# A convolution's last tap applied to the block and to the running sum, and an evacuation and weight casts issued behind the last square

## The chip, the cores and the metric

One core of one Trainium2 chip runs the whole kernel; no other core takes part. The metric is the device time of one execution in microseconds (us). Each time shown is the median of several runs. One further execution was recorded by the hardware profiler; its page and its trace are what the text quotes. In them PE is TensorE's matrix unit, PEld its loading of weights, DVE is VectorE, ACT is ScalarE, POOL is GpSimd and SP is SyncE, which issues the DMAs. "L1501" is line 1501 of the kernel.

## The reference

The input is one sequence of 1024 tokens with 1024 channels. Layer 0 (a state space model beside retention) is not touched. Layer 1 is a gated Conformer convolution, with the norms around it:

```
def mixer_conv(h, w_in, conv_w, conv_b, ln_g, ln_b, w_out):
    proj = h @ w_in
    a, b, g = jnp.split(proj, 3, axis=-1)
    u = a * jax.nn.sigmoid(b)
    u = lax.conv_general_dilated(u, conv_w[:, None, :], ...)     # causal, depthwise, width CONV_K = 31
    u = u + conv_b
    mu = jnp.mean(u, axis=-1, keepdims=True)
    var = jnp.mean(jnp.square(u - mu), axis=-1, keepdims=True)
    u = (u - mu) * lax.rsqrt(var + EPS) * ln_g + ln_b
    u = jax.nn.silu(u) * jax.nn.silu(g)
    return u @ w_out

x = x + mixer_conv(rmsnorm(x, norm_g[1]), ...)
out = rmsnorm(x, final_g)
```

Everything is float32. The mean and the variance are taken over all 1024 channels of a token, so the last of the channels must be through the convolution before any of them can be normalised.

## The kernel before

**Layout.** Channels lie on the 128 partitions and time on the free axis. The 1024 channels make 8 blocks (KB), and the 1024 tokens are worked on as two halves of 512 (HALF), so that a tile is 128 x 512. A product in float32 is done as three products of a reduced type: each operand is split into a high and a low part, and `mm3` multiplies high weights by high data (L181), high weights by low data (L182) and low weights by high data (L183). One output block of 128 x 512 takes 8 steps of three matmuls, 24 in all, into one PSUM bank. There are three such banks ("mm"). The high part of a block of weights is cast on ScalarE (L171, or L148 where a block is loaded a second time) and the low part is a subtraction on GpSimd (L172), or for the second half a load of what the first half stored. Weights are fetched two blocks ahead (`wnext`), three buffers for each part.

**What runs around the change.** The end of the kernel has these pieces, for the first half (h = 0) and the second (h = 1):

- `conv(h, n2)`: the taps of two blocks. A few go to ScalarE and GpSimd (L1477, L1478); the others are instructions of VectorE (L1501), each of which multiplies a shifted slice of `u` by a weight per channel and adds it to an accumulator in a bank. For blocks 4 to 7 an estimate of the mean, `pilot`, is subtracted ahead of the last tap (L1494). The last tap writes its result to a tile `co` in SBUF.
- `conv_sums`: GpSimd adds the blocks up, one sum over the values (`cs`, L1542) and one over their squares (`cq`, L1544), each a 128 x 512 tile. ScalarE makes the squares (`csquare`).
- `conv_norm`: for the second half VectorE adds block 7 to the sum (L1551) and block 7's square, which ScalarE leaves in a bank `cvq_bank`, to the sum of squares (L1552). `conv_norm_wide` then sums each over the partitions with one product with a matrix of ones (`wide_sums`, L487), which leaves the two statistics `cst0` and `cst1` in two banks, spread over all partitions. The variance (L1584, L1588), the mean (L1587) and the reciprocal root (`wide_rsqrt`: a table load L495, Ln L497, Exp L498 and Square L499 on ScalarE, L500 and L501 on VectorE) follow.
- `conv_scale`: per block the value is scaled, the mean's part subtracted, Silu applied (L1605 on ScalarE), the gate multiplied in (L1611), and the result split into `zh` (a cast on ScalarE, L1232) and `zl` (a subtraction, L1234). The eight pairs are the operands of the second half's output products.
- `w_out_c(h, nb)`: one output block: 24 matmuls into a bank `mm_oc`, the evacuation on VectorE that adds the residual (L1635), its square on ScalarE (L1636), the sum of squares on GpSimd (L1640) and a scaling on ScalarE (L1641).

**What sets the order.** A scheduler places each engine's instructions by priorities (`self.at(n)`, the lower number first) and by when their inputs are there; `self.tc.issue_after(ins)` adds an edge, so that what is inside is issued behind `ins`. Each engine then works through its own queue in order. The output blocks of the first half fill TensorE while the second half's norm is on the other engines: blocks 0 to N0 - 1 are emitted ahead of it. Blocks N0 to 7 are emitted behind it, with `hold`: a dictionary that says from which of the 8 steps on a block's matmuls are issued behind a given instruction. Here `norm_mm`, the second statistic, stands between steps 0 and 1 of block 5:

```
N0, HOLD = 5, 1
...
    def gemm_seq(self, ps, seq, hold=None):
        with ExitStack() as held:
            for i, (w, xs, kb) in enumerate(seq):
                if hold and i in hold:
                    held.enter_context(self.tc.issue_after(hold[i].ins))
                self.mm3(ps, w, kb, (xs[kb][0][:], xs[kb][1][:]), i == 0, i == len(seq) - 1)
```

The functions that the diff touches, and what calls them:

Of the kernel before, what the change touches and what calls it, by code (L numbers as in the profile page):

```python
# [11 lines left out]
F32 = mybir.dt.float32  # L12
F32R = mybir.dt.float32r
I32 = mybir.dt.int32
AF = mybir.ActivationFunctionType
ALU = mybir.AluOpType
# [3 lines left out]
P = 128  # L20
D = 1024
T = 1024
KB = 8
HALF = 512
NH = 8
EPS = 1e-6
CONV_K = 31
MAGIC = 12582912.0
N0, HOLD = 5, 1
WARM = 14  # L30
RMM = 5
IDLE = 4
# [20 lines left out]
class Trunk:  # L53
# [1182 lines left out]
    def layer0_back_and_layer1(self, st):  # L1236
        nc, A = self.nc, self.A
        v, gp = nc.vector, nc.gpsimd
# [3 lines left out]
        ps_cv = self.pool("ps_cv", 2, PSUM, stack=st)  # L1242
# [96 lines left out]
        for i, x in ((6, t2), (7, t3), (4, t4)):  # L1339
            for m in range(2):  # L1340
                w = wn()
# [122 lines left out]
        def conv(h, n2):  # L1464


            accs_, outs, us, s0s = [], [], [], []
            late = h == 0 and n2 == 0
            for nb in (n2, n2 + 1):
                u = ub[h][nb]  # L1470
                with self.at(105000 + 100000 * h + 100 * nb):
                    s0 = lp.tile([P, HALF], F32, name=f"tp{nb}_{h}_0", tag="tp", bufs=3)
                    nc.scalar.activation(s0[:], u[:, 0:HALF], AF.Identity, scale=cw[:, nb, 0:1],
                                         bias=self.vec(V_CB, nb))
                    for k in range(1, NT[h]):
                        sk = lp.tile([P, HALF], F32, name=f"tp{nb}_{h}_{k}", tag="tp", bufs=3)
                        nc.scalar.mul(sk[:], u[:, k:k + HALF], cw[:, nb, k:k + 1])  # L1477
                        gp.tensor_tensor(s0[:], s0[:], sk[:], op=ALU.add)  # L1478
                us.append(u)
                s0s.append(s0)  # L1480
                acc = ps_cv.tile([P, HALF], F32, name=f"cv{nb}_{h}", tag="cv")
                if not late:
                    with self.at(105000 + 100000 * h + 100 * nb):
                        nc.scalar.copy(acc[:], s0[:])  # L1484
                accs_.append(acc)
                outs.append(opB.tile([P, HALF], F32, name=f"co{nb}_{h}", tag="B0"))
            for k in range(NT[h], CONV_K):
                for i, nb in enumerate((n2, n2 + 1)):
                    dst = outs[i] if k == CONV_K - 1 else accs_[i]
                    tap = us[i][:, k:k + HALF], cw[:, nb, k:k + 1]  # L1490
                    if k == CONV_K - 1 and late:
                        v.tensor_tensor(accs_[i][:], accs_[i][:], s0s[i][:], op=ALU.add)
                    if k == CONV_K - 1 and n2 >= 4:
                        v.tensor_tensor(accs_[i][:], accs_[i][:], pilot[h][:], op=ALU.subtract)  # L1494

                    ahead = (h, n2) == (0, 6) and k >= NORM_TAP[i]
                    if k == NT[h] and late:
                        v.tensor_scalar(dst[:], *tap, None, op0=ALU.mult)
                        continue
                    with self.tc.issue_after(self.norm_first.ins) if ahead else nullcontext():  # L1500
                        v.scalar_tensor_tensor(dst[:], *tap, accs_[i][:], op0=ALU.mult, op1=ALU.add)  # L1501
            cv[h][n2:n2 + 2] = outs
# [14 lines left out]
        def csquare(h, nb, bank=None):  # L1517
            sq = bank or (self.opA.tile([P, HALF], F32, name=f"cvq{nb}_{h}", tag="A1") if h else
                  lp.tile([P, HALF], F32, name=f"cvq{nb}_{h}", tag="sq", bufs=1))
            nc.scalar.activation(sq[:], cv[h][nb][:], AF.Square)  # L1520
            return sq

        def conv_center(h):
# [21 lines left out]

        def conv_norm(h):
            sm, acc = accs[("cv", h)]

            q7 = csquare(h, 7, h and ps_cv.tile([P, HALF], F32, name="cvq_bank", tag="cv"))
            e = v if h else gp  # L1550
            e.tensor_tensor(sm[:], sm[:], cv[h][7][:], op=ALU.add)  # L1551
            e.tensor_tensor(acc[:], acc[:], q7[:], op=ALU.add)  # L1552
            if h:
                return conv_norm_wide(sm, acc)
            st = ps_cv.tile([P, HALF], F32, name=f"cst_{h}", tag="cn")
            s1, s2 = st[:, 0:256], st[:, 256:512]
            self.token_sums([(s1, sm[:]), (s2, acc[:])])
            st4 = st[:].rearrange("p (k b x) -> p k b x", k=2, x=64)

            t4 = [lp.tile([P, 4], F32, name=f"cn4_{i}_{h}", tag=f"cn4_{i}", bufs=1) for i in range(4)]  # L1560
            d4, q4, v4, r4 = (t[:] for t in t4)
            nc.scalar.activation(q4, st4[:, 0, :, 0], AF.Square, scale=1.0 / D)
            nc.scalar.mul(d4, st4[:, 0, :, 0], 1.0 / D)
            v.scalar_tensor_tensor(v4, st4[:, 1, :, 0], 1.0 / D, q4, op0=ALU.mult, op1=ALU.subtract)
            self.rsqrt(r4, v4)
            v.tensor_tensor(d4, d4, r4, op=ALU.mult)
            Rp = ps_cv.tile([P, HALF], F32, name=f"cR_{h}", tag="cn")
            self.spread_split(Rp[:], r4, lp, f"cR_{h}")
            Dp = ps_cv.tile([P, HALF], F32, name=f"cD_{h}", tag="cn")
            with self.tc.issue_after(self.last_diag.ins):  # L1570
                self.spread_split(Dp[:], d4, lp, f"cD_{h}")
            dl = lp.tile([P, HALF], F32, name=f"dl_{h}", tag="cs", bufs=1)
            nc.scalar.copy(dl[:], Dp[:])
            conv_scale(h, Rp, dl)

        def conv_norm_wide(sm, acc):

            s1, s2 = (ps_cv.tile([P, HALF], F32, name=f"cst{i}_1", tag="cn") for i in range(2))
            self.wide_sums(s1[:], sm[:])
            self.wide_sums(s2[:], acc[:])  # L1580
            self.norm_mm = self.last_stat

            m2 = lp.tile([P, HALF], F32, name="cm2_1", tag="dg", bufs=1)
            self.squared = nc.scalar.activation(m2[:], s1[:], AF.Square, scale=1.0 / D)  # L1584
            dl = lp.tile([P, HALF], F32, name="dl_1", tag="cs", bufs=1)
            with self.tc.issue_after(self.squared.ins):
                nc.scalar.mul(dl[:], s1[:], 1.0 / D)  # L1587
            v.scalar_tensor_tensor(s2[:], s2[:], 1.0 / D, m2[:], op0=ALU.mult, op1=ALU.subtract)  # L1588
            self.wide_rsqrt(s2[:], lp, "cn_1")
            v.tensor_tensor(dl[:], dl[:], s2[:], op=ALU.mult)  # L1590
            conv_scale(1, s2, dl)
# [23 lines left out]
                zs[h][nb] = (a, b)  # L1615

        final = [[], []]

        def w_out_c(h, nb, cols, hold=None):

            w = self.wnext(f"woc{nb}_{h}")
            tag, bufs = ("tp", 3) if h and nb > 4 else ("ld", 2)
            xt = lp.tile([P, HALF], F32, name=f"x1l{nb}_{h}", tag=tag, bufs=bufs)
            with self.tc.issue_after(self.early_low.ins) if h and nb > 4 else nullcontext():
                nc.sync.dma_start(xt[:], self.x1_d[rows(nb), hs(h)])
            t = self.opA.tile([P, HALF], F32, name=f"x2_{nb}_{h}", tag=f"A{h}")
            sq = lp.tile([P, HALF], F32, name=f"s2q{nb}_{h}", tag="sacc" if nb == 0 else "ev",
                         bufs=1 if nb == 0 else 3)
            final[h].append((t, sq))

            def part(c):
                ps = self.bank(f"mm_oc{nb}_{h}_{c.start}", aux=False)
                n = c.stop - c.start
                self.gemm(ps[:, :n], w, [(a[:, c], b[:, c]) for a, b in zs[h]], hold)
                self.last_add = v.tensor_tensor(t[:, c], ps[:, :n], xt[:, c], op=ALU.add)  # L1635
                self.squared = nc.scalar.activation(sq[:, c], t[:, c], AF.Square)  # L1636

                if 0 < nb < KB - (h == 1 and c.start > 0):
                    a = final[h][0][1]
                    gp.tensor_tensor(a[:, c], a[:, c], sq[:, c], op=ALU.add)  # L1640
                nc.scalar.mul(t[:, c], t[:, c], self.vec(V_FG, nb))  # L1641
            for c in cols:
                yield part(c)
# [49 lines left out]
        for h in range(2):  # L1693
# [15 lines left out]
            def blocks(h, nbs, hold={}):  # L1709
                for nb in nbs:  # L1710
                    for _ in w_out_c(h, nb, full, hold.get(nb)):
                        pass

            with self.at(400000):
                if h == 0:
                    blocks(0, range(N0))
                    continue
                blocks(0, range(N0, 8), {N0: {HOLD: self.norm_mm}, N0 + 1: {0: self.norm_mm}})
            with self.at(410000):
                blocks(1, range(3))  # L1720
                with self.tc.issue_after(self.last_mm.ins):
# [123 lines left out]
```

## Time and profile before

| | before |
|---|---|
| median of three runs | 1184.66 us (1184.64 to 1185.43) |
| the profiled execution | 1186.61 us |
| its span | 1184.8 us |
| PE (TensorE) busy | 1171.0 us, 99% of the span |
| DVE (VectorE) busy | 847.0 us, 71% |
| POOL (GpSimd) busy | 655.4 us, 55% |
| ACT (ScalarE) busy | 490.0 us, 41% |
| mean granted clock of TensorE | 0.996 |

How to read the rows that follow. A row of single instructions gives start, duration, engine, line, operation, output<-inputs, the tile's shape and type, and in brackets how long the engine was idle ahead of it and what ended that wait; "x5" stands for five like instructions in a row. In the chain of waits each row is a start, a share of time and the engine, tile and line that the end of the program waited for then. In the view by stretches each engine has its busy time with the count of instructions; PEclk is the granted clock of TensorE, as a share of full speed. A busy PE is not PE at its peak: at a lower clock the same matmul is busy for longer.

### The profile page before, as it was taken

To read this page: it belongs to the slowest core of one execution; us is meant where nothing else is said; L and a number is where in the kernel's file an instruction comes from. 1 tells how busy PE (TensorE), PEld (TensorE's weight loads), DVE (VectorE), ACT (ScalarE), POOL (GpSimd) and SP (SyncE) were. 2 spreads that over 40 slices of the span, in tenths; PEclk is the share of its full clock that TensorE was granted. 3 is DMA by queue.
4 is the path that set the end of the run, shared out by engine and by line. 5 is a ranking of instruction groups with operands and counts; after the bars stand their busy time and mean duration, and the time that the engine had idled before them with its cause. 6 is when DMAs were issued, how large, how long until landed. Compare 5 with 4: busy or idle time off the path is not lost.

```text
span 1184.8 us, 17218 instructions
## 1 busy us (share of the span) xinstructions
PE 1171.0 (99%) x6286; PEld 979.9 (83%) x6286; DVE 847.0 (71%) x1463; ACT 490.0 (41%) x719; POOL 655.4 (55%) x448
## 2 busy tenths in 40 slices
PE   9999999999999999999999999999999999999897
PEld 7888888888888889999888888888888888888676
DVE  7975698777417359586679324599999799899643
ACT  6422232322223231333456325445536675344673
POOL 2059999888145354233572111687525577667643
PEclk9999999999999999999999999999999999999899
DMA  9344345555387667779998977656668554367664
GB/s 350 107 135 136 126 153 170 183 174 187 109 279 259 246 224 210 248 230 361 366 340 288 322 269 237 220 196 215 223 224 303 199 203 142 110 212 272 207 243 148
DMA packets 117637, 261.46 MB, mean 221 GB/s; under 512 B 10672, under 2 KB 42288, under 8 KB 116912
## 3 DMA queue, kind: packets, MB, share of 16 engines
q1 hardware_dynamic: 117552, 260.36, 65.0%
q8 instruction: 49, 0.80, 0.3%
q14 instruction: 36, 0.29, 0.1%
HBM read 181.48 MB, written 74.65 MB: 216 GB/s over the span
## 4 chain that ended last, share of the span: by engine, by line
PE 89%; DMA 3%; DVE 3%; ACT 1%; issue 1%; POOL 1%; SPq 1%; POOLq 0%; DVEq 0%; ACTq 0%
PE mm_g L181 8%; PE mm_g L182 7%; PE mm_g L183 7%; PE mm_wo L182 5%; PE mm_wo L183 5%; PE mm_wo L181 5%; PE mm_b L182 2%; PE mm_a L182 2%; PE mm_b L181 2%; PE mm_a L181 2%; PE mm_b L183 2%; PE mm_a L183 2%; PE mm_glu L181 2%; PE mm_glu L182 2%; PE mm_glu L183 2%; PE mm_oc L182 2%
## 5 line engine op out<-in xcount | busy, mean ns | idle before, releaser
L1501 DVE SCALAR_TENSOR_TENSOR cv<-u,convw,cv 128x512 f32<-128x512 f32 x398 | 273.1, 749 | 11.6 <-ACT cv L1484 9.7
L1478 POOL TENSOR_TENSOR tp<-tp,tp 128x512 f32<-128x512 f32 x64 | 83.8, 1309 | 36.5 <-ACT tp L1477 35.5
L181 PE MATMUL mm_g<-xh,wh_g 128*128 128x512 f32 x256 | 101.8, 398 | 0.0
L183 PE MATMUL mm_g<-xh,wl_g 128*128 128x512 f32 x256 | 100.1, 391 | 0.0
L182 PE MATMUL mm_g<-xl,wh_g 128*128 128x512 f32 x256 | 100.0, 391 | 0.0
L415 POOL TENSOR_TENSOR s1q<-s1q,s1q 128x512 f32<-128x512 f32 x12 | 17.7, 1477 | 86.1 <-ACT s1q L410 86.1
L1477 ACT ACTIVATE tp<-u,convw 128x512 f32<-128x512 f32 x64 | 45.3, 718 | 34.7 <-POOL tp L1478 34.6
L181 PEld LDWEIGHTS mm_g<-xh,wh_g 128*128 128x128 f32 x256 | 48.0, 188 | 11.7 <-issue 1.2
L183 PEld LDWEIGHTS mm_g<-xh,wl_g 128*128 128x128 f32 x256 | 48.1, 188 | 10.4
L182 PEld LDWEIGHTS mm_g<-xl,wh_g 128*128 128x128 f32 x256 | 48.1, 188 | 9.9 <-issue 0.4
L371 DVE TENSOR_TENSOR gt<-mm_g,R 128x512 f32<-128x512 f32 x32 | 21.8, 683 | 45.5 <-PE mm_g L183 45.5
L181 PE MATMUL mm_oc<-zh,wh_woc 128*128 128x512 f32 (+1 forms) x144 | 53.9, 379 | 0.0
L182 PE MATMUL mm_oc<-zl,wh_woc 128*128 128x512 f32 (+1 forms) x144 | 53.1, 370 | 0.2 <-POOL zl L1234 0.2
L183 PE MATMUL mm_oc<-zh,wl_woc 128*128 128x512 f32 (+1 forms) x144 | 52.8, 369 | 0.0
L172 POOL TENSOR_TENSOR wl_v<-wf_v,wh_v 128x1024 fp32r<-128x1024 f32 x12 | 31.2, 2611 | 38.5 <-ACT wh_v L171 38.5
L172 POOL TENSOR_TENSOR wl_glu<-wf_glu,wh_glu 128x1024 fp32r<-128x1024 f32 x14 | 34.0, 2428 | 33.0 <-ACT wh_glu L171 26.6
L181 PE MATMUL mm_wo<-ysh,wh_wos 128*128 128x512 f32 x128 | 50.2, 392 | 0.0
L181 PE MATMUL mm_g<-h1h,wh_cg 128*128 128x512 f32 x128 | 50.2, 392 | 0.0
L183 PE MATMUL mm_b<-h1h,wl_cb 128*128 128x512 f32 x128 | 49.9, 390 | 0.0
L182 PE MATMUL mm_b<-h1l,wh_cb 128*128 128x512 f32 x128 | 49.8, 389 | 0.0
L182 PE MATMUL mm_wo<-ysl,wh_wos 128*128 128x512 f32 x128 | 49.8, 389 | 0.0
L182 PE MATMUL mm_a<-h1l,wh_ca 128*128 128x512 f32 x128 | 49.8, 389 | 0.0
(523 smaller groups left out, 3652.5 us busy)
## 6 DMA issues: line engine op xcount, KB each, us to landing
wf_g<-w_ab SPq DMA_DIRECT2D x16, 512.0 KB
wf_wos<-w_out SPq DMA_DIRECT2D x16, 512.0 KB
wf_wor<-w_out SPq DMA_DIRECT2D x16, 512.0 KB
wf_cb<-w_c SPq DMA_DIRECT2D x16, 512.0 KB
wf_ca<-w_c SPq DMA_DIRECT2D x16, 512.0 KB
wf_woc<-w_out_c SPq DMA_DIRECT2D x16, 512.0 KB
wf_v<-w_v SPq DMA_DIRECT2D x12, 512.0 KB
wf_cg<-w_c SPq DMA_DIRECT2D x11, 512.0 KB
```

What stands on the lines that cost most here:

```text
L172: self.low_made = lo[i].tensor_tensor(wl[:].rearrange(fl)[:, c], wf[:, c], h.bitcast(F32), op=ALU.subtract)
L181: nc.tensor.matmul(ps, wh[:, kb, :], xh, start=start, stop=False, **more)
L182: nc.tensor.matmul(ps, wh[:, kb, :], xl, start=False, stop=False, **more)
L183: self.last_mm = nc.tensor.matmul(ps, wl[:, kb, :], xh, start=False, stop=stop, **more)
L371: nc.vector.tensor_tensor(gt[:, c], ps[:], self.R[:, c], op=ALU.mult)
L415: nc.gpsimd.tensor_tensor(a, a, sq[:], op=ALU.add)
L1477: nc.scalar.mul(sk[:], u[:, k:k + HALF], cw[:, nb, k:k + 1])
L1478: gp.tensor_tensor(s0[:], s0[:], sk[:], op=ALU.add)
L1501: v.scalar_tensor_tensor(dst[:], *tap, accs_[i][:], op0=ALU.mult, op1=ALU.add)
```

## The change

The change does four things, all of them near the second half's norm.

- The last tap of the second half's block 7 is no longer issued in `conv`. Its operands are kept in `self.last_tap`, and `conv_norm_wide` issues three instructions of VectorE: `total` = accumulator + old sum, into a bank (`cvs_bank`); `co` = tap + accumulator, as before; and the new sum = tap + `total`. The last tap is thus applied twice, to the block and to the sum. The sum's addition of `co` (L1551) goes. The square of block 7 and its addition follow, and that addition is remembered as `squares_added`.
- N0 goes from 5 to 4: block 4 of the first half is emitted behind the norm, without a hold. Its evacuation is issued behind `squares_added`.
- Blocks 5 to 7 of the first half (their loads and casts with them, as far as they are fetched there) are issued behind ScalarE's square of block 7, `last_square`.
- HOLD goes from 1 to 2: the second statistic stands between steps 1 and 2 of block 5, and ahead of block 6.

For the first half the statements are only moved within `conv_norm`.

```diff
-N0, HOLD = 5, 1
+N0, HOLD = 4, 2
...
+                    if (h, nb, k) == (1, KB - 1, CONV_K - 1):
+                        self.last_tap = *tap, accs_[i], dst
+                        continue
...
-            nc.scalar.activation(sq[:], cv[h][nb][:], AF.Square)
+            self.squared = nc.scalar.activation(sq[:], cv[h][nb][:], AF.Square)
...
-            q7 = csquare(h, 7, h and ps_cv.tile([P, HALF], F32, name="cvq_bank", tag="cv"))
-            e = v if h else gp
-            e.tensor_tensor(sm[:], sm[:], cv[h][7][:], op=ALU.add)
-            e.tensor_tensor(acc[:], acc[:], q7[:], op=ALU.add)
             if h:
                 return conv_norm_wide(sm, acc)
+            q7 = csquare(h, 7)
+            gp.tensor_tensor(sm[:], sm[:], cv[h][7][:], op=ALU.add)
+            gp.tensor_tensor(acc[:], acc[:], q7[:], op=ALU.add)
...
         def conv_norm_wide(sm, acc):
+            u, w, part, co = self.last_tap
+            total = ps_cv.tile([P, HALF], F32, name="cvs_bank", tag="cv")
+            v.tensor_tensor(total[:], part[:], sm[:], op=ALU.add)
+            v.scalar_tensor_tensor(co[:], u, w, part[:], op0=ALU.mult, op1=ALU.add)
+            v.scalar_tensor_tensor(sm[:], u, w, total[:], op0=ALU.mult, op1=ALU.add)
+            q7 = csquare(1, 7, ps_cv.tile([P, HALF], F32, name="cvq_bank", tag="cv"))
+            self.last_square = self.squared
+            self.squares_added = v.tensor_tensor(acc[:], acc[:], q7[:], op=ALU.add)
...
-                self.last_add = v.tensor_tensor(t[:, c], ps[:, :n], xt[:, c], op=ALU.add)
+                behind = self.behind.pop(nb, None)
+                with self.tc.issue_after(behind.ins) if behind else nullcontext():
+                    self.last_add = v.tensor_tensor(t[:, c], ps[:, :n], xt[:, c], op=ALU.add)
...
-                blocks(0, range(N0, 8), {N0: {HOLD: self.norm_mm}, N0 + 1: {0: self.norm_mm}})
+
+                self.behind = {N0: self.squares_added}
+                blocks(0, range(N0, N0 + 1))
+
+                with self.tc.issue_after(self.last_square.ins):
+                    blocks(0, range(N0 + 1, 8), {N0 + 1: {HOLD: self.norm_mm}, N0 + 2: {0: self.norm_mm}})
```

More of the change, by code (lines that the diff above doesn't have):

```diff
@@ L1617, in layer0_back_and_layer1 @@
         final = [[], []]
+        self.behind = {}
         def w_out_c(h, nb, cols, hold=None):
```

## The prediction, made before the changed kernel ran

> **What bounds the kernel now.** I read the page first, then the busy time by stage, the chain of waits, and the timelines of the engines around the one stage that the diff touches. Every time below is in us from the start of the profiled span.
>
> ```profile
> span 1184.8 us, 17218 instructions
> PE 89%; DMA 3%; DVE 3%; ACT 1%; issue 1%; POOL 1%; SPq 1%; POOLq 0%; DVEq 0%; ACTq 0%
> ```
>
> TensorE carries 89% of the chain that ends last, so a change is worth what it takes out of TensorE's idle time or gives back in its clock. The stages show where there is something to take.
>
> ```profile
> core 0: us, PE busy (x), PEclk, DMA share, GB/s
> 1085.00:1103.28 18.28, 18.28 (x81) 1.00 0.95 324
> 1103.28:1107.21 3.93, 0.00 (x1) 0.92 0.81 294
> 1107.21:1113.38 6.17, 6.17 (x11) 0.50 0.52 174
> 1113.38:1134.60 21.22, 21.22 (x94) 1.00 0.60 199
> ...
> 1174.88:1178.33 3.45, 2.74 (x17) 1.00 0.89 304
> ```
>
> TensorE stands still for 3.93 us at 1103.28, and the granted clock is 0.50 until 1113.38 behind it. The 0.92 of the idle stretch puts the drop at 1106.6: 0.08 x 3.93 / 0.5 = 0.63 us before its end. So the clock fell 3.3 us into the pause and stayed at half for 6.8 us. In the fourth row 94 matmuls take 21.22 us, 0.226 us each. The last row has 0.71 us of idle time in 3.45 and the clock stays at 1.00. The chain of waits tells who caused the pause:
>
> ```profile
> 1103.32 0.69 DVE x L1635
> 1104.01 0.67 DVE co L1501
> 1104.77 2.40 DVE cs L1551
> 1107.21 3.78 PE cst L487 x4
> 1110.99 0.43 PE mm_oc L181
> ...
> 1113.12 0.40 PE mm_oc L183
> 1113.53 0.23 PE mm_oc L181
> ...
> 1124.58 3.86 DMA wf_woc<-w_out_c
> ...
> 1144.64 0.86 PE rf_R L487 x2
> ```
>
> VectorE first evacuates block 4 (L1635), then runs the last tap (L1501), then adds it to the running sum (L1551); only then can the two statistics (cst) run. Two like passes take 0.86 us at full clock (last row), so the four at 3.78 us lose 2.06, and the six matmuls from 1110.99 to 1113.53 lose 2.54 - 6 x 0.226 = 1.18. One more wait follows in this stage:
>
> ```profile
> 1102.89 0.39 PE L183 MATMUL mm_oc<-zh,wl_woc 128*128 128x512 f32 x1
> 1134.82 0.50 PE L182 MATMUL mm_oc<-zl,wh_woc 128*128 128x512 f32 x1 [0.19 <-POOL zl L1234]
> ```
>
> The loss now is 3.93 + 2.06 + 1.18 + 0.19 = 7.36 us. That is the most that the change can win here.
>
> **The change part by part.** All instructions up to 1085 are the same and stand in the same order; I walk the queues from there, in the order in which the changed kernel's instructions stand on each engine, with the durations of these rows.
>
> ```profile
> 1096.26 0.75 DVE L1501 SCALAR_TENSOR_TENSOR cv<-u,convw,cv 128x512 f32<-128x512 f32 x1
> 1097.20 0.69 DVE L1635 TENSOR_TENSOR x<-mm_oc,x1l 128x512 f32<-128x512 f32 x1 [0.20 <-PE mm_oc L183]
> 1097.81 3.91 DVE L1501 SCALAR_TENSOR_TENSOR cv<-u,convw,cv 128x512 f32<-128x512 f32 x5
> 1101.76 0.70 DVE L1494 TENSOR_TENSOR cv<-cv,pilot 128x512 f32<-128x512 f32 x1
> 1103.32 0.69 DVE L1635 TENSOR_TENSOR x<-mm_oc,x1l 128x512 f32<-128x512 f32 x1 [0.86 <-PE mm_oc L183]
> 1103.93 0.74 DVE L1501 SCALAR_TENSOR_TENSOR co<-u,convw,cv 128x512 f32<-128x512 f32 x1
> 1104.77 2.39 DVE L1551 TENSOR_TENSOR cs<-cs,co 128x512 f32<-128x512 f32 x1
> 1107.08 0.68 DVE L1552 TENSOR_TENSOR cq<-cq,cvq_bank 128x512 f32<-128x512 f32 x1
> 1098.15 2.41 POOL L172 TENSOR_TENSOR wl_woc<-wf_woc,wh_woc 128x1024 fp32r<-128x1024 f32 x1 [0.44 <-ACT wh_woc L171]
> 1104.26 2.35 POOL L172 TENSOR_TENSOR wl_woc<-wf_woc,wh_woc 128x1024 fp32r<-128x1024 f32 x1 [1.20 <-ACT wh_woc L171]
> ```
>
> The last tap twice. The old sum takes 2.39 us where L1552 takes 0.68; it ends at 1107.16, 0.55 us after GpSimd's L172 (1104.26 + 2.35). That is a wait for GpSimd. It reads two tensors from SBUF. The new form is one addition (accumulator in a bank plus the old sum, into a bank) and two taps, each with one SBUF tensor and one bank. Nothing shows exactly this addition; the nearest rows are L1494 and L1552 at 0.70 and 0.68, and the worst is the 2.39. I take 0.70, because five such taps run in 3.91 us at 1097.81, which is 0.66 from start to start, while L172 of 1098.15 is at work. VectorE gains one instruction, 0.66, and loses a stall of 1.71.
>
> Evacuations and casts behind. No evacuation stands ahead of the last tap any more: block 3's cost 0.20 + 0.61 there and block 4's 0.86 + 0.61. The pilot's subtraction then ends near 1101.6, the three new instructions follow at 0.6 to 0.7, and the sum is ready at 1103.6 instead of 1107.16. TensorE has six matmuls of block 5 ahead of the statistics where there were three, so it is done at 1103.28 + 3 x 0.226 = 1103.96 and starts the first statistic without a wait. The evacuation of block 3 now stands between the new sum and the addition of the squares, and TensorE computes the rest of block 3 last: it starts at 1104.00, the addition of the squares runs 1104.61 to 1105.28, and the second statistic starts at 1105.33 where the first ended at 1103.96 + 0.86 = 1104.82. That is a new wait of 0.51, too short for the clock to fall if it takes 3.3 as above. The statistics end at 1106.19 instead of 1110.99. TensorE then has 66 matmuls of the first half left and comes to the second half's blocks at 1121.1; now it comes there at 1113.53 + 63 x 0.226 = 1127.8. The lead is 6.7 us.
>
> What is late next. The second half's operands hang on ScalarE, whose queue the moved work now enters:
>
> ```profile
> 1103.14 1.04 ACT L171 CAST wh_woc<-wf_woc 128x1024 fp32r<-128x1024 f32 x1 [3.26 <-PE mm_oc L182]
> 1104.10 0.63 ACT L1636 ACTIVATE s2q<-x 128x512 f32<-128x512 f32 x1
> 1105.23 0.71 ACT L1641 ACTIVATE x<-x,vecs 128x512 f32<-128x512 f32 x1
> 1109.81 0.59 ACT L1587 ACTIVATE dl<-cst 128x512 f32<-128x512 f32 x1
> 1110.42 1.28 ACT L495 ACT_TABLE_LOAD   x1
> 1111.84 0.69 ACT L497 ACTIVATE cn_dg<-cst,epst 128x512 f32<-128x512 f32 x1
> 1112.56 0.63 ACT L498 ACTIVATE cn_dg<-cn_dg 128x512 f32<-128x512 f32 x1
> 1113.22 0.63 ACT L499 ACTIVATE cn_sq<-cn_dg 128x512 f32<-128x512 f32 x1
> 1116.81 1.06 ACT L148 CAST wh_woc<-wf_woc 128x1024 fp32r<-128x1024 f32 x1 [2.96 <-PE mm_oc L182]
> 1128.62 0.59 ACT L1232 CAST zh<-zz 128x512 fp32r<-128x512 f32 x1
> ```
>
> Now L495 to L499 run back to back and end at 1113.85. In the changed order the scaling of block 3 and the square of block 4 stand between L495 and L497, the scaling of block 4 between L497 and L498, and a cast of weights between L498 and L499. One starts 0.09 before the one ahead of it ends (1103.14 + 1.04 against 1104.10), so these cost 0.62 + 0.54 + 0.62 + 0.96 = 2.74. With the cast of the seventh weights, the square of block 3 and L1584 and L1587 ahead of it, L495 starts at 1106.4; L497 follows at 1108.75, L498 at 1109.98, and L499 ends at 1112.1. Of the 4.8 us that the statistics won, this chain keeps 1.75.
>
> From there to the cast of the third operand of the second half (the row at 1128.62) it is 14.8 us now. In the changed order ScalarE has 19 instructions on that way instead of 16: a cast more for the cast that went ahead of L499, the square and scaling of block 7 (0.54 + 0.62) and one more Silu. But the 2.96 us in which it waits for TensorE ahead of the row at 1116.81 are gone. My walk gives 15.0: cast at 1127.2, ready at 1127.8. TensorE has 18 matmuls to do with the first two operands, from 1121.1 to 1125.2, and then must wait: 2.6 us in all. Part of it, up to 0.8, falls on the low half of the third weights, whose load is issued when block 7 is done, at 1121.3, and takes 3.86 by the row of wf_woc; that is inside the 2.6. Later operands come ahead of their use but for 0.1. SP's loads of x1 for the second half stand ahead of two low halves of weights that are now issued before them; the walk has them landed some 4 us before use, so I cost that at nothing.
>
> The sum. The changed kernel loses 0.5 + 2.6 + 0.1 = 3.2 where 7.36 were lost: 4.1 us less. The profiled execution took 1186.61 us, 1.8 of them outside its span of 1184.8: by the sum the span becomes 1180.7 and that execution 1182.5. It lay 1.95 above the median of the runs shown, 1184.66, and the same 4.1 off the median gives **1180.6**.
>
> Both ends. If the third operand comes no earlier than now (ready at 1129.2), the wait is 4.0 and the gain 2.7: 1182.0. If ScalarE's queue costs nothing and only the 0.51 stays, the gain is 6.85: 1177.8. I take the walk, since it uses rows of the same instructions.
>
> **Rivals.** The clock falls again. The clock needs a pause; it fell 3.3 us into the old one, and the new pause is 2.6 us in two pieces with some 0.9 us of matmuls between. If that is enough, 6.8 us at half clock cost 3.4 and the gain is 0.7: 1184.0. Against it: 2.6 is under 3.3 and is broken, and the last row of the stages has 0.71 of idle time at a clock of 1.00. [...]
>
> The lead turns into one long wait (slower). Place: ScalarE's queue between L497 and the third cast, where the square of block 7 waits for an evacuation that VectorE does among the operands. The pause reaches 3.3 us, and the half clock with it, when the operand is ready at 1128.5, 0.7 later than my walk; pause and clock then eat all, and from there each us is a us lost. Ready at 1131.3, the pause is 6.1, and 7.36 - 0.5 - 6.1 - 3.4 = -2.6: 1187.3. Against it: it needs 3.5 us more than rows of the same instructions give.
>
> The sum is not sooner. The two taps and the addition could be held by GpSimd as L1551 is. Then the first statistic starts at 1107.1 again, the clock falls as before, and only the three matmuls ahead are won: 1184.0. The taps beside L172 speak against it.
>
> ScalarE's insertions fall into gaps. Then the gain is near 6: 1178.5. Its queue has no gap of that size in the walk.
>
> **How the numbers follow.** The forecast has 0.67 with a range of its own of 1179.4 to 1182.2; the clock 0.14; the long wait 0.05; the sum not sooner 0.06; the larger gain 0.08. About 0.2%, 2.4 us, is what a measurement of this kernel can tell from no change. Forecast and larger gain are faster (0.75); clock and sum are the same, but for 0.01 that ends slower (0.19); the rest is slower (0.06). The range for 8 in 10 reaches to the larger gain below and to the two cases at 1184.0 above: 1178.9 to 1184.1.
>
> **What would show it.** The wait of cst for VectorE of 3.9 is gone, with 0.5 in its place for the squares; the granted clock stays at 1.00 between 1100 and 1150; L499 ends about 1.7 earlier than at 1113.85; a wait of TensorE for zh of about 2 us appears near 1126; the passes of rf_R start near 1140.5. I am wrong if the clock shows 0.50 again in this stage, if the first statistic still waits, or if the pause at the third operand is over 3.3.

## The result, and the profile after

Over 22 runs of each kernel the changed kernel takes 1184.14 us (median; 1182.25 to 1185.92) and the kernel before, in the same session, 1186.04 (1184.56 to 1188.80). The ratio is 0.9981, with a 95% interval of 0.9974 to 0.9987: faster by 2.3 us, or 1.9 by the medians, where 4.1 were forecast. The profiled execution took 1182.88 us. Its page begins:

```profile
span 1181.1 us, 17216 instructions
PE 1169.7 (99%) x6286; PEld 979.1 (83%) x6286; DVE 848.4 (72%) x1464; ACT 490.0 (41%) x719; POOL 654.7 (55%) x448
```

The span of this execution was forecast at 1180.7 and is 0.4 above it; the median was forecast at 1180.6 and is 3.5 above it. That execution and the median thus tell two different stories, and the sections below are about the difference. First the stage in the profiled execution, in stretches as before:

```profile
core 0: us, PE busy (x) PEld busy (x) DVE busy (x) ACT busy (x) POOL busy (x), PEclk, DMA share, GB/s
1085.00:1103.69 18.69, 18.69 (x83) 15.21 (x83) 17.39 (x26) 6.98 (x10) 12.26 (x7) 1.00 0.85 292
1103.69:1106.29 2.60, 2.25 (x6) 0.94 (x6) 1.89 (x3) 2.58 (x5) 1.57 (x1) 1.00 0.98 338
1106.29:1125.87 19.58, 19.58 (x85) 15.19 (x83) 12.46 (x19) 17.11 (x25) 15.15 (x13) 1.00 0.82 272
1125.87:1128.34 2.47, 0.17 (x1) 0.00 (x0) 1.38 (x3) 2.47 (x5) 2.47 (x3) 1.00 0.89 304
1128.34:1140.76 12.42, 12.42 (x55) 10.17 (x55) 5.34 (x8) 5.56 (x9) 4.60 (x4) 1.00 0.06 18
```

TensorE's pause of 3.93 at 1103.28 is gone. In its place stand a short wait between the two statistics (second row) and a pause ahead of 1128.34 (fourth row). The clock is 1.00 throughout. The timeline of the same execution, a few rows of each engine, names the waits:

```profile
1101.63 0.70 DVE L1583 TENSOR_TENSOR cvs_bank<-cv,cs 128x512 f32<-128x512 f32 x1
1102.24 0.74 DVE L1584 SCALAR_TENSOR_TENSOR co<-u,convw,cv 128x512 f32<-128x512 f32 x1
1102.89 0.74 DVE L1585 SCALAR_TENSOR_TENSOR cs<-u,convw,cvs_bank 128x512 f32<-128x512 f32 x1
...
1103.69 1.13 PE L487 MATMUL cst<-cs,ones 128*128 128x512 f32 x2
1105.17 1.12 PE L487 MATMUL cst<-cq,ones 128*128 128x512 f32 x2 [0.35 <-DVE cq L1588]
1111.26 0.63 ACT L499 ACTIVATE cn_sq<-cn_dg 128x512 f32<-128x512 f32 x1
1115.71 1.06 ACT L148 CAST wh_woc<-wf_woc 128x1024 fp32r<-128x1024 f32 x1 [0.41 <-DMA wf_woc<-w_out_c]
1127.72 0.57 ACT L1232 CAST zh<-zz 128x512 fp32r<-128x512 f32 x1
1128.34 0.96 PE L181 MATMUL mm_oc<-zh,wh_woc 128*128 128x512 f32 x3 [2.30 <-ACT zh L1232]
1140.76 1.02 PE L487 MATMUL rf_R<-s2q,ones 128*128 128x512 f32 x2
```

The three new instructions take 0.70 to 0.74, the sum is ready before TensorE wants it, and the one long wait is that for the third operand (zh), 2.30, at the place where the walk had it. From the first output product to rf_R the stage took 1144.48 - 1075.24 = 69.24 us in the profile that the prediction was made from, and takes 1140.76 - 1075.07 = 65.69 here: 3.55 less, of 4.1 forecast.

### The profile page after: what moved, and what is told of

Same layout as the page of the kernel before. It is cut to its first block, busy times and chain, and to the rows that moved or that the text cites. A ratio compares the mean times of both kernels' runs of the same rounds, so it can differ in the third digit from the quotient of the medians.

```text
span 1181.1 us, 17216 instructions
## 1 busy us (share of the span) xinstructions
PE 1169.7 (99%) x6286; PEld 979.1 (83%) x6286; DVE 848.4 (72%) x1464; ACT 490.0 (41%) x719; POOL 654.7 (55%) x448
## 4 chain that ended last, share of the span: by engine, by line
PE 96%; ACT 1%; DVE 1%; DMA 1%; issue 1%; POOL 0%; POOLq 0%; ACTq 0%
PE mm_g L181 8%; PE mm_g L183 7%; PE mm_g L182 7%; PE mm_wo L181 5%; PE mm_wo L182 5%; PE mm_wo L183 5%; PE mm_b L183 2%; PE mm_b L181 2%; PE mm_a L181 2%; PE mm_a L183 2%; PE mm_a L182 2%; PE mm_b L182 2%; PE mm_u L181 2%; PE mm_u L183 2%; PE mm_u L182 2%; PE mm_glu L181 2%
## 5 line engine op out<-in xcount | busy, mean ns | idle before, releaser
L172 POOL TENSOR_TENSOR wl_glu<-wf_glu,wh_glu 128x1024 fp32r<-128x1024 f32 x14 | 34.0, 2428 | 32.9 <-ACT wh_glu L171 20.2
L172 POOL TENSOR_TENSOR wl_v<-wf_v,wh_v 128x1024 fp32r<-128x1024 f32 x12 | 31.2, 2603 | 35.0 <-ACT wh_v L171 35.0
L183 PE MATMUL mm_g<-h1h,wl_cg 128*128 128x512 f32 x128 | 49.8, 389 | 0.0
```

The source lines that it names most:

```text
L172: self.low_made = lo[i].tensor_tensor(wl[:].rearrange(fl)[:, c], wf[:, c], h.bitcast(F32), op=ALU.subtract)
L183: self.last_mm = nc.tensor.matmul(ps, wl[:, kb, :], xh, start=False, stop=stop, **more)
```

## The experiments

### Both kernels once more: the clock is not the same in every execution

The kernel before, unchanged:

> The kernel before, unchanged, to see how its executions spread. Theory 1 (the clock's fall behind TensorE's pause is not in every execution): the mean granted clock takes at least two values over the executions, near 0.996 where it fell for 6.8 us and near 0.999 where it didn't, and the executions without the fall are 2 to 3 us shorter. Theory 2 (it falls in every execution, the spread has another origin): one value of the clock near 0.996, whatever the span. Median about 1186 by both.

The changed kernel, unchanged:

> The changed kernel, unchanged, for the spread and a second profile. Theory 1 (the clock falls behind one of the new short pauses in part of the executions): the mean clock is 0.999 in about half of them with a span near 1181.2, and 0.997 in the others with a span of 1182.5 or more; a profile of the second kind shows a stretch at 0.50 of up to 6.8 us that starts behind the statistics or at the third operand. Theory 2 (noise in loads or elsewhere): the clock is the same where the span differs. Ratio to before 0.998 by both.

Measured: 1185.95 us (11 runs, ratio to the kernel before of the same session 1.0003, interval 0.9994 to 1.0012) and 1184.36 (11 runs, 0.9985, 0.9976 to 0.9994). The second profile of the kernel before, in stretches:

```profile
core 0: us, PE busy (x) PEld busy (x) DVE busy (x) ACT busy (x) POOL busy (x), PEclk, DMA share, GB/s
1103.56:1107.49 3.93, 0.01 (x1) 0.00 (x0) 3.78 (x4) 2.67 (x4) 2.94 (x2) 1.00 0.80 299
1107.49:1108.67 1.18, 1.18 (x3) 0.67 (x4) 0.55 (x1) 0.01 (x1) 1.09 (x1) 1.00 0.86 337
1108.67:1112.09 3.42, 3.42 (x8) 2.00 (x7) 0.70 (x1) 3.36 (x5) 0.00 (x0) 0.50 0.64 198
```

The pause is the same 3.93 us, but the clock falls 1.18 us after its end and stays at half for 3.41 us (3.42 in the row, by rounding); in the profile that the prediction used it fell inside the pause and stayed for 6.83. The second profile of the changed kernel:

```profile
core 0: us, PE busy (x) PEld busy (x) DVE busy (x) ACT busy (x) POOL busy (x), PEclk, DMA share, GB/s
1125.76:1128.09 2.33, 0.00 (x0) 0.00 (x0) 1.38 (x3) 2.33 (x5) 2.33 (x3) 1.00 0.93 317
1128.09:1128.59 0.50, 0.50 (x2) 0.46 (x3) 0.50 (x1) 0.50 (x2) 0.50 (x1) 0.94 0.48 184
1128.59:1132.01 3.42, 3.42 (x9) 2.60 (x9) 2.57 (x5) 2.25 (x4) 3.42 (x4) 0.51 0.01 2
1132.01:1142.08 10.07, 10.07 (x45) 8.28 (x45) 2.28 (x4) 2.81 (x4) 0.64 (x1) 1.00 0.04 11
```

Here nearly the same pause as in the first profile of the changed kernel (2.33 against 2.30) is followed by 3.41 us at half clock. In these three profiles the half clock lasts 6.83, 3.41 and 3.41 us, and starts 3.27, 5.11 and 2.77 us behind the beginning of the pause.

The traces show where. The thirteen profiles of this case hold 18 falls of the clock, five in this stage and one at the end of each execution. In the five executions with both, the two start 75.09 us apart (before, first), 71.70 (before, second), 51.20 (after, second), 71.68 (the sum alone) and 51.20 (the order alone, both in the next section): 22, 21, 15, 21 and 15 units of 3.413. In the first profiles of the two kernels the three falls also start 1102.51, 1177.60 and 1170.77 us, or 323, 345 and 343 such units, after the clock's first rise. So the time of these executions can be cut into units with fixed borders, in the other profiles counted back from the fall at the end, and a pause of TensorE falls into them one way in one execution and another way in the next. The two closest cases are the first profile of the changed kernel,

```profile
core 0: us, PE busy (x), PEclk, DMA share, GB/s
1126.52:1129.93 3.41, 1.59 (x7) 1.00 0.59 222
1129.93:1133.34 3.41, 3.41 (x17) 1.00 0.02 5
```

and that of the order alone:

```profile
1128.04:1131.45 3.41, 1.48 (x6) 1.00 0.58 200
1131.45:1134.86 3.41, 3.41 (x9) 0.50 0.02 5
```

The first row of each is the unit that holds most of the pause, the second is the unit behind it. The units of this stage with the most idle time, over all profiles, are these (the versions with one part alone are described further down):

| profile | longest pause | unit | TensorE busy in it, of 3.41 | clock in the next unit |
|---|---|---|---|---|
| before, first | 3.93 | 1103.14 to 1106.55 | 0.14 | half |
| sum alone | 2.69 | 1103.44 to 1106.85 | 0.83 | half |
| after, second | 2.33 | 1125.12 to 1128.53 | 1.07 | half |
| before, second | 3.93 | 1105.26 to 1108.67 | 1.18 | half |
| order alone | 2.21 | 1128.04 to 1131.45 | 1.48 | half |
| sum alone, late scalings | 2.70 | 1103.92 to 1107.33 | 1.57 | full |
| after, first | 2.30 | 1126.52 to 1129.93 | 1.59 | full |

Over the whole of all thirteen traces, from the first rise on, all 18 falls stand behind a unit with at least 1.93 us of idle time, and no unit with 1.84 or less is followed by one. In the first profile of the kernel before, the clock came back only behind a unit without idle time; the unit with 0.66 was followed by another at half.

The mean clock of each execution says how often this happens. The thirteen profiles also lose 0.9 to 2.2 us of full clock at the very end, behind TensorE's last product, where it costs nothing. So no fall in our stage shows as 0.999 or 0.998, one unit as 0.998 or 0.997, and two as 0.996 or less. The executions at 0.998, 13 of the kernel before and 4 of the changed one, are put down to one unit here because their medians, 1185.35 and 1184.45, are close to those of the executions at 0.997, 1185.45 and 1184.38; that is argued, not shown.

| mean clock | before, 81 executions | median us | after, 33 executions | median us |
|---|---|---|---|---|
| 0.996 and 0.995 (two units) | 33 | 1186.21 | 0 | |
| 0.997 and 0.998 (one unit) | 48 | 1185.41 | 20 | 1184.40 |
| 0.999 (none) | 0 | | 13 | 1182.93 |

Theory 1 holds in the main: the kernel before loses one unit or two, the changed kernel one in 20 of 33. It had also expected executions of the kernel before without a fall, and there are none. The frequencies fit the units: a pause of 3.93 has at least half of itself, 1.96, in one unit wherever it lies. For a pause of 2.33, an estimate from the border (1.89, the middle of 1.84 and 1.93), with every place in a unit equally likely, is (3.41 + 2.33 - 2 x 1.89) / 3.41 = 0.57; 20 of 33 is 0.61.

### The sum alone, the order alone

The sum alone is the changed kernel with the old order:

```diff
-N0, HOLD = 4, 2
+N0, HOLD = 5, 1
...
-                self.behind = {N0: self.squares_added}
-                blocks(0, range(N0, N0 + 1))
-                with self.tc.issue_after(self.last_square.ins):
-                    blocks(0, range(N0 + 1, 8), {N0 + 1: {HOLD: self.norm_mm}, N0 + 2: {0: self.norm_mm}})
+                blocks(0, range(N0, 8), {N0: {HOLD: self.norm_mm}, N0 + 1: {0: self.norm_mm}})
```

> Only the last tap is applied twice; N0, HOLD and the order of the evacuations and casts are as before. If the gain comes from the sum: VectorE's addition of 2.39 us is gone, TensorE's pause ahead of the first statistic shrinks from 3.9 to about 2.2 us, the clock falls in fewer executions, and the profiled execution without a fall is about 3.7 us shorter than before's 1186.6 (1182.9). If the gain comes from the order alone: the pause stays above 3 us and the time within 1 us of before.

The order alone keeps the change's order and has the old sum (the last tap as it was in `conv`):

```diff
-            u, w, part, co = self.last_tap
-            total = ps_cv.tile([P, HALF], F32, name="cvs_bank", tag="cv")
-            v.tensor_tensor(total[:], part[:], sm[:], op=ALU.add)
-            v.scalar_tensor_tensor(co[:], u, w, part[:], op0=ALU.mult, op1=ALU.add)
-            v.scalar_tensor_tensor(sm[:], u, w, total[:], op0=ALU.mult, op1=ALU.add)
...
+            v.tensor_tensor(sm[:], sm[:], cv[1][7][:], op=ALU.add)
```

> Only the order: N0 4, HOLD 2, block 4's evacuation behind the squares, loads and casts behind the last square; the sum is the old addition of two tensors in SBUF. If the old addition is held by GpSimd wherever it stands, it takes about 2.4 us and TensorE pauses about 2 to 3 us ahead of the first statistic, time 1 to 2 us above the changed kernel. If the order alone takes it out of GpSimd's way, it takes 0.7, the pause is about 1.2, and the time is within 1 us of the changed kernel.

Measured: the sum alone 1183.93 us (0.9982, 0.9974 to 0.9991), as fast as the whole change; the order alone 1185.52 (0.9996, 0.9987 to 1.0004), no gain. The timeline of the sum alone:

```profile
1104.30 2.36 POOL L172 TENSOR_TENSOR wl_woc<-wf_woc,wh_woc 128x1024 fp32r<-128x1024 f32 x1 [1.21 <-ACT wh_woc L171]
1104.57 0.74 DVE L1584 SCALAR_TENSOR_TENSOR co<-u,convw,cv 128x512 f32<-128x512 f32 x1
1105.23 0.74 DVE L1585 SCALAR_TENSOR_TENSOR cs<-u,convw,cvs_bank 128x512 f32<-128x512 f32 x1
1106.02 1.28 PE L487 MATMUL cst<-cs,ones 128*128 128x512 f32 x2 [2.69 <-DVE cs L1585]
```

GpSimd's L172 is at work from 1104.30 to 1106.66, and the new sum, one bank and one SBUF tensor, still takes 0.74 beside it, where the old one took 2.39. That step of the prediction is shown. The pause shrinks from 3.93 to 2.69, where about 2.2 was expected. The timeline of the order alone:

```profile
1105.20 0.68 DVE L1579 TENSOR_TENSOR cs<-cs,co 128x512 f32<-128x512 f32 x1
...
1105.94 1.13 PE L487 MATMUL cst<-cs,ones 128*128 128x512 f32 x2 [1.38 <-DVE cs L1579]
1129.97 0.97 PE L181 MATMUL mm_oc<-zh,wh_woc 128*128 128x512 f32 x3 [2.21 <-ACT zh L1232]
```

Here the old addition of two SBUF tensors takes 0.68: in this order L172 starts only at 1105.49, 0.29 behind it, and then takes 2.62 itself, where it takes 2.40 and 2.41 earlier in this trace. So in these traces the old sum is dear where it meets an L172 that is already at work (2.39) and not where it starts ahead of one (0.68); both parts of the change avoid that, each in its way. But this order brings the pause at the third operand, and in this profile the clock was at half for 3.41 us from 1131.45. The forecast "within 1 us of the changed kernel" missed: it is 1.2 above the 1184.36 of the same session.

### The pause taken away

The pause hangs on ScalarE's queue by the prediction. In the first run the scalings of the first half's blocks 4 to 7, which nobody needs before 1140, stand behind the last cast of the second half's operands (`last_cast` is the cast of zh in `split`):

```diff
...
+                if (h, nb) == (1, 7):
+                    self.scale_behind = self.last_cast
...
-                nc.scalar.mul(t[:, c], t[:, c], self.vec(V_FG, nb))
+                late = h == 0 and nb >= 4
+                with self.tc.issue_after(self.scale_behind.ins) if late else nullcontext():
+                    nc.scalar.mul(t[:, c], t[:, c], self.vec(V_FG, nb))
```

> The changed kernel, with the scalings of the first half's blocks 4 to 7 on ScalarE issued behind the last cast of the second half's operands, out of the chain that makes them. If the pause at the third operand comes from ScalarE's queue, the third operand no longer makes TensorE wait; the next limit is GpSimd, whose subtraction for the fourth operand then makes TensorE wait some 1.6 us at 1130. Theory 1 (the clock falls when a pause fills enough of a window of 3.4 us): with 1.6 instead of 2.3 it falls in fewer executions than the changed kernel's 20 of 33; the fall decides more than the pause itself. Time without a fall about 1182.7, 0.3 below the changed kernel without one (1182.97). Rival (any short pause is enough): it falls as often as before, median 1184.

Measured: 1182.09 us (7 runs, 1181.73 to 1182.62; ratio 0.9968, 0.9957 to 0.9980). Its waits of TensorE, line by line (waiting line, releaser, total, count, longest):

```profile
PE mm_oc L182 <- POOL zl L1234: 1.5, 1, 1.5
PE rf_ps L444 <- ACT s2q L1652: 0.6, 1, 0.6
PE cst L487 <- DVE cq L1588: 0.4, 1, 0.4
```

The wait for zh is gone, and GpSimd's zl is next with 1.53, as expected. No execution shows less than 0.998, all lie within 0.9 us, and the profiled one has no fall in the stage; no unit of it has more than 0.84 us of idle time there. It is 0.8 below the changed kernel's executions without a fall (1182.93) and 2.3 below those with one. The 0.8 would be the pause's 2.33 - 1.53, but that isn't shown: the changed kernel ran in other sessions, and the kernel before took 1185.46 in this one against 1185.86 and 1186.04 in those.

The second run also moves GpSimd's sums of squares of blocks 6 and 7 (`last_low` is the subtraction of zl in `split`):

```diff
...
+                if (h, nb) == (1, 3):
+                    self.sum_behind = self.last_low
...
-                    gp.tensor_tensor(a[:, c], a[:, c], sq[:, c], op=ALU.add)
+                    with self.tc.issue_after(self.sum_behind.ins) if h == 0 and nb >= 6 else nullcontext():
+                        gp.tensor_tensor(a[:, c], a[:, c], sq[:, c], op=ALU.add)
```

> The same, and GpSimd's sums of squares of the first half's blocks 6 and 7 issued behind the fourth operand's subtraction. By the walk no pause of TensorE between 1085 and 1145 is over 0.6 us; the three left add up to about 1.1. Theory 1: the clock falls in no execution in this stage, all executions are near 1181.4, 2.7 below the changed kernel's median and 4.5 below the kernel before. Rival (the pause was not what made the clock fall, or the time is bound elsewhere): median 1182.5 or more and falls as often as in the changed kernel.

Measured: 1182.08 us (6 runs, 0.9971, 0.9959 to 0.9982). Its waits of TensorE up to rf_R:

```profile
PE mm_oc L181 <- ACT zh L1232: 0.8, 1, 0.8
PE cst L487 <- DVE cq L1588: 0.4, 1, 0.4
```

No pause is over 0.8, and no execution shows a mean clock under 0.998. The time was forecast at 1181.4; it is 0.7 higher and no lower than the run before, although its stage is shorter in the profiles (64.28 against 65.01 us). The two profiles also differ ahead of the stage: the first output product starts at 1075.98 and at 1074.84. A gain of 0.7 can be lost in that spread.

The third fills the wait between the statistics with one step of block 5:

```diff
             self.wide_sums(s1[:], sm[:])
+            self.norm_sum = self.last_stat
             self.wide_sums(s2[:], acc[:])
...
-                    blocks(0, range(N0 + 1, 8), {N0 + 1: {HOLD: self.norm_mm}, N0 + 2: {0: self.norm_mm}})
+                    blocks(0, range(N0 + 1, 8), {N0 + 1: {HOLD: self.norm_sum, HOLD + 1: self.norm_mm}, N0 + 2: {0: self.norm_mm}})
```

> The same as the run before, and one step of block 5 between the two statistics, so that the wait for the addition of the squares (0.35 in the changed kernel's trace) is filled. Expected: 0.35 to 0.6 us less than the run before, about 1180.9, and no wait of cst for cq. If the filled wait only reappears at the second half's operands: the same time as the run before.

Measured: 1181.91 us (5 runs, 0.9966, 0.9953 to 0.9978), and again:

> The version with no long pause once more, against kernels of the same call: median 1181.5 to 1182.0, ratio 0.996 to 0.997.

Measured: 1181.24 us (5 runs, 0.9964, 0.9951 to 0.9976). The first of the two has one wait of TensorE left in the stage:

```profile
1126.15 0.96 PE L181 MATMUL mm_oc<-zh,wh_woc 128*128 128x512 f32 x3 [0.83 <-ACT zh L1232]
```

The wait for cq is gone, as expected; the second profile shows 0.67 for zh, 0.47 for the sum and 0.25 for a load. The first median missed its forecast: it is 0.17 below that of the run before, where 0.35 to 0.6 was expected, and within the noise the two are the same. This version has the lowest median measured: 3.6 and 4.4 us below the kernel before in the same sessions. The changed kernel was 1.9 and 1.5 below it in its own two.

### Is the order part worth nothing?

The sum alone, with the late scalings (here of blocks 5 to 7) and late sums of squares of above, N0 5 and HOLD 1:

> Only the last tap applied twice, N0, HOLD and the order of evacuations and casts as before, with the late scalings and the late sums of squares of the two runs above. If the order part of the change is worth nothing (as the run of the sum alone seems to say): as fast as the run with both parts, about 1181.4. If the order part only moved the pause: TensorE keeps the pause of 2.7 us ahead of the first statistic, the clock falls there in most executions, and the time is 0.9 (without a fall) to 2.6 us (with one) above the run with both parts.

Measured: 1182.83 us (9 runs, 1181.22 to 1185.74; 0.9978, 0.9969 to 0.9988). Its profiled execution had no fall, and this one wait:

```profile
1105.76 1.12 PE L487 MATMUL cst<-cs,ones 128*128 128x512 f32 x2 [2.70 <-DVE cs L1585]
```

Four of the nine executions lie at 1183.4 to 1185.7 with a clock of 0.997, the other five at 1181.2 to 1182.8, level with the version of both parts. So the order part moves a pause rather than takes it away: without it TensorE pauses 2.7 us at the statistics, with it 2.3 at the third operand, and either makes the clock fall in a part of the executions. Once the third operand is early, the order is worth 0.75 by the medians (1182.83 against 1182.08). The intervals of the two ratios overlap; the four executions at 0.997 are what sets the two versions apart.

The pause of that version can be cut with HOLD 3 for 1:

> The last tap applied twice, the late scalings and late sums of squares, the old order with N0 5, and HOLD 3 for 1. The pause of 2.7 us ahead of the first statistic becomes about 1.4, with two waits of 0.3 at the operands. Theory 1: no fall in this stage in any execution, no executions above 1183 as the run with HOLD 1 had five of nine (1182.83 to 1185.74); median near 1181.8. Rival (the falls there had another cause): executions above 1183 again in about half.

Measured: 1182.82 us (11 runs, 0.9978, 0.9969 to 0.9986). Its waits of TensorE were 1.14 and 0.89, and nine of the eleven executions lie at 1181.8 to 1182.9. The profiled one, without a fall, took 1183.59, and one took 1186.39 at a clock of 0.998; what lengthened the last isn't known. So the slow executions are mostly gone, against the rival, but the median did not come down to 1181.8, and why is open: the waits add up to 2.03 us against 2.70 in the profile with HOLD 1, yet from the first product to rf_R it took 65.20 against 64.58.

### One number changed in the kernel before

```diff
-N0, HOLD = 5, 1
+N0, HOLD = 5, 5
```

> The kernel before with one number changed, HOLD 5 for 1: the statistics stand behind five steps of block 5, so that TensorE has 12 more matmuls (2.7 us) ahead of them and 12 fewer behind. No wait is removed by it, only moved: by the walk the 3.9 us ahead of the first statistic become about 1.4, and three waits of 1.0 to 1.6 us come at the second half's operands. If the clock decides (theory 1), it falls in few executions, since no pause fills half of 3.4 us, and the time drops by about 2.5 us, to 1183.5, as far as with the whole change. If the waits decide, whose sum stays at 4 to 5 us: no gain, 1185.5 or more.

Measured: 1183.97 us (11 runs, 1183.28 to 1185.14; 0.9985, 0.9976 to 0.9994). Its waits of TensorE:

```profile
1122.45 0.97 PE L181 MATMUL mm_oc<-zh,wh_woc 128*128 128x512 f32 x3 [1.72 <-ACT zh L1232]
1128.08 0.96 PE L181 MATMUL mm_oc<-zh,wh_woc 128*128 128x512 f32 x3 [0.98 <-ACT zh L1232]
1132.17 0.50 PE L182 MATMUL mm_oc<-zl,wh_woc 128*128 128x512 f32 x1 [0.95 <-POOL zl L1234]
```

and its stretches from the statistics to rf_R:

```profile
1105.65:1107.20 1.55, 1.55 (x6) 0.78 (x5) 0.69 (x1) 1.30 (x2) 0.18 (x1) 1.00 0.20 77
1107.20:1120.73 13.53, 13.53 (x59) 10.68 (x57) 7.09 (x11) 12.35 (x18) 8.37 (x6) 1.00 0.79 291
1120.73:1122.45 1.72, 0.00 (x2) 0.00 (x1) 1.50 (x4) 1.72 (x4) 1.72 (x3) 1.00 0.18 33
1122.45:1141.82 19.37, 17.44 (x72) 13.23 (x73) 10.50 (x16) 11.38 (x18) 12.16 (x10) 1.00 0.27 97
```

The waits still add up to 3.65 us, against 3.93 + 0.19 before; that at the statistics, forecast at 1.4, is gone. None is over 1.72, no unit of 3.41 has more than 1.00 of idle time, the clock stays at 1.00, and no execution shows less than 0.998. The time is as low as with the whole change. From the first product to rf_R its profiled execution takes 66.55 us, no less than the kernel before does without its half clock (66.16 and 66.19, below). So the waits gave nothing, and the drop of 1.8 us by the ratio is the clock's.

## Why the prediction was partly right and its number wrong

**The sum (right).** The three instructions cost 0.70 to 0.74 each and are not held by GpSimd; the rival that they would be is refuted by the run of the sum alone, where the two taps run wholly beside L172 and the addition in part. The first statistic started at 1103.69 without a wait (forecast 1103.96), the second after 0.35 (forecast 0.51).

**What is late next (right, its size 0.5 short).** TensorE came to the second half at 1121.19 (forecast 1121.1), and L499 ended at 1111.89 (forecast 1112.1). The third operand was ready at 1128.3 where 1127.8 was forecast. One piece of this is a cast that waited 0.41 for a load of weights at 1115.71, which the walk had on time. Besides, the 18 products of the first two operands started late by small amounts between 1120.91 and 1125.65: 4.74 us for 18 starts that take 4.08 at 0.227 each, 0.66 in all. With the wait of 2.30 and 0.1 lost among the products behind it that is about 3.1, where the forecast had 2.6. That ScalarE's queue sets the third operand is shown by the run with the late scalings, in which the wait for it is gone.

**"The clock fell 3.3 us into the pause" (wrong).** This was the step that failed. The prediction read a duration out of one execution and used it twice: the fall needs a pause of 3.3 us, so 2.6 is safe; and the old fall costs 3.24, to be won in full. The 3.3 was no threshold. It is the part of the pause (3.27) that lay ahead of the border of a unit; the second profile of the kernel before has the same pause and a fall 1.18 us behind its end, and the second profile of the changed kernel has a fall with a pause of 2.33. That is the 0.50 in this stage which the prediction named as a sign of being wrong; the first profile does not show it.

The rival "the clock falls again" was there, with a chance of 0.14 and a price of 3.4 (6.8 us at half clock). It happens in 20 of 33 executions and costs 1184.40 - 1182.93 = 1.5, since there it is one unit of 3.41. That its time, 1184.0, is close to the measured 1184.14 is luck: it was worked out from 1184.66 for the kernel before, with a fall of two units in every execution.

**The clock's term (mis-sized).** The profile at hand was an execution with two units. It lay 1.95 above the median of the runs shown; the prediction saw the distance and carried it over as an offset. The clocks of those runs aren't on record, but one unit for two (1.4 by the costs that follow) would explain most of it. The two units cost 6.17 / 2 = 3.09 there, since 0.66 of the 6.83 us lay in the pause, and one unit behind the pause costs 3.41 / 2 = 1.71. With 48 of 81 executions at one unit and 33 at two, the kernel before loses about 2.3 us on the mean (an estimate: the cost of two is that of one profile, and by the medians of the classes the second unit costs 0.8 rather than 1.4). The changed kernel loses 20/33 of 1.71, or 1.0. So the clock gives about 1.2 us, not 3.24. What the waits give is read from the four profiles of the stage, with the clock's loss taken out, which is half of the time in which TensorE worked at half clock:

| profile | first product to rf_R | at work at half clock | without the loss |
|---|---|---|---|
| before, first | 69.24 | 6.17 | 66.16 |
| before, second | 67.90 | 3.41 | 66.19 |
| after, first | 65.69 | 0 | 65.69 |
| after, second | 67.24 | 3.41 | 65.53 |

The waits give 0.5 to 0.7, where 7.36 - 3.24 - 3.2 = 0.9 was forecast. Clock and waits together are 1.7 to 1.9, and 1.9 to 2.3 was measured.

**The baseline.** 1180.6 was worked out from 1184.66, the median of three runs; 22 gave 1186.04. From that the same 4.1 would have been 1181.9, still 2.2 too low. The rivals of one long wait and of insertions that fall into gaps did not come true.

## What to carry to other kernels

One profile showed one draw of the clock here (two units at half in 33 of 81 executions of the kernel before, one in 48): before a half clock is priced, look at the mean clock of all executions, or take a second profile, and price the fall by its frequency. In this case what counted was TensorE's idle time within one unit of 3.41 us (a fall behind 1.93 or more, none behind 1.84 or less), so a pause that is split in pieces, at a nearly unchanged sum (3.65 against 4.12), was worth as much as the whole change. And when a wait goes, ask on which queue the next one hangs: here it was ScalarE and then GpSimd, both busy with work that nobody needed before the stage was over.

## What the runs showed of the hardware that was not expected

- In the stage the half clock lasted 3.41 us in four profiles and 6.83 in one, and the falls of an execution lay 15 to 22 units of 3.413 apart. A fall followed a unit in which TensorE had idled 1.93 us or more (18 of 18 falls in thirteen profiles) and none in which it had idled 1.84 or less. The longest pause alone does not decide: 2.33 brought a fall in one profile where 2.70, split over two units, brought none in another. By the mean clock, a pause of 2.3 brought a fall in 20 of 33 executions and one of 3.93 in all 81. With longest pauses of 1.72 or less no profile shows a fall in the stage, though one execution, that of 1186.39, stands out unexplained. Whether a border between 1.84 and 1.93 holds for other kernels was not tried.
- The same addition of two SBUF tensors took 2.39 us beside a running L172 of GpSimd and 0.68 where it started ahead of L172, in the same stage; with one operand in a bank the addition took 0.69, half of it beside L172, and the taps behind it 0.74 each, all of it beside L172.
- Ahead of the stage, TensorE runs the same products in the same order in all versions, and yet the stage's first product starts anywhere from 1074.81 to 1076.25 in the thirteen profiles, 1.4 us, more than some of the effects looked for.
